# An expert with 96 slots instead of 128, in a two-layer mixer with a top-2 mixture of experts

## The chip, the cores and the metric

The kernel runs on one core of one Trainium2 chip. The metric is device microseconds of one execution; the median of three executions is given with the lowest and the highest.

## The reference

256 tokens and 256 context tokens of width 1024 go through two layers. Each layer mixes tokens (window attention beside a chunked mLSTM) and then channels: layer 0 by a dense SwiGLU of width 2816, layer 1 by a mixture of eight such SwiGLUs. All is float32. The part that the change touches is the mixture:

```python
N_EXPERTS, TOP_K, FFN_DIM = 8, 2, 2816

def swiglu(t, w1, w3, w2):
    return (jax.nn.silu(t @ w1) * (t @ w3)) @ w2

def moe_swiglu(h, w_router, b_router, w1, w3, w2):
    t = h.reshape(-1, shp[-1])                       # 256 x 1024
    logits = (t @ w_router).astype(jnp.float32) + b_router
    top_v, top_i = lax.top_k(logits, TOP_K)
    top_w = jax.nn.softmax(top_v, axis=-1)
    combine = sum over the two of one_hot(top_i) * top_w
    y = sum over e of combine[:, e] * swiglu(t, w1[e], w3[e], w2[e])
```

Each token uses two of eight experts, so 512 places fall to the eight, 64 to each on the mean.

## The kernel before

**Precision.** Every float32 operand of a large product is kept as two fp32r tiles, H (rounded) and L (the rest). `mm3` does three matmuls for one product: aH with bH, aH with bL, aL with bH. Weights come from HBM in blocks of 1 MB (`raw`), and `_split_tile` makes H on ScalarE (L123) and L on VectorE or GpSimd (L124). All matmuls go through `Timed.matmul` (L227) and `Timed.transpose` (L231), so they share those two lines; the tile names tell them apart. In these names the second operand is the stationary one: `ps_mm<-H,X` streams the weight tile H past the stationary tile X.

**The weights' order.** The program is first run once without a chip to log the order in which blocks are used; then `Weights` issues loads (L388 among others, on SyncE's queue) as buffers come free and splits blocks ahead of their use. The generators of a stage (`weave`, `take`) and an agenda (`soon(n, f)` puts f n beats later, `beat()` counts) set the order in which everything else is issued. Each engine then runs its own instructions in that order.

**The mixture.** After the router, `pos` holds for every token and expert the number of earlier tokens of that expert, and `A` whether the token uses it. `onehot` writes from them a matrix of 128 tokens x 128 slots: one where the token has that slot. An expert then works on its slots only:

- `gather(e0)` makes X for two experts at once: `rows_in` multiplies 128 tokens' rows (stationary, `tt`) with the one-hot columns of both experts (`Pt`, 2 x 128 columns streamed) for each of 8 chunks of the width, in bank `ps_t` (the first gather in several banks), and ScalarE and VectorE scale it and split it to XH and XL (L1593 to L1595). Pair 0 is gathered ahead of the experts, pairs 2, 4 and 6 inside the odd experts.
- `expert` computes the two first products with the slots as stationary columns: for six blocks of 512 columns (the last 256) of w1 and w3, 8 chunks x `mm3` into `ps_mm`. `finish` takes silu (L1618) and the product (L1619); some beats after, `later` transposes the result, `sa`, 128 columns at a time into `ps_t` (L231), and copies it to hH (ScalarE, L1633) and hL (VectorE, L1634). Then 22 chunks of w2 are multiplied with hH and hL (stationary) into two banks `ps_s`.
- the result is scaled (`ys`, L1666), split (`y`), and `combine` spreads it to the tokens with the transposed one-hot matrix `PTm` (L1562, made in `slots_t`), into the running sum `yacc` (L1679). The last expert does the same in the outer `finish`, and `result` normalizes and stores.

Work of one expert is issued under that of another: the gather of the next pair, the transposes and the scatter stand between the matmuls of w1, w3 and w2 in TensorE's queue.

**The general path.** Should an expert have more than 128 tokens, a block behind the test below runs a loop over all experts for slots 128 to 255 and normalizes again:

```python
    ncnt = nc.values_load(cnt[0:1, 0:1], min_val=0, max_val=T)
    with tc.If(ncnt > cap):
```

Of the kernel before, what the change touches and what calls it, by code (L numbers as in the profile page):

```python
# [8 lines left out]
F32 = mybir.dt.float32  # L9
# [4 lines left out]
OP = mybir.AluOpType  # L14
# [254 lines left out]

def emit(ctx, tc, I, out, order=None, log=None, dbg=None, stop=None, cap=128):  # L270
    nc = tc.nc
# [1140 lines left out]
    for tag, key in zip(("hH", "hL"), HK):  # L1412
        W.add_pool(mo, 1, lambda k, key=key: k == key, (tag, NF * 128))
    W.add_pool(mo, RAW2, late)
# [58 lines left out]
    Pt = ap_.tile([128, 1024], F32R, tag="aL0", name="Pt")  # L1473
    Pp = [Pt[:, i * 512:(i + 1) * 512].rearrange("p (b e q) -> p b e q", b=2, e=2) for i in range(2)]
    W.add_pool(ap_, 1, late, ("aL1", 2048, True))
# [68 lines left out]
    PTm = cst.tile([128, 2, T], F32R, tag="sqacc", name="PTm")  # L1544

    def onehot(dst, b, pcol, acol, shift=0):
        if shift:
            V.tensor_scalar(dst, iota, float(shift), pcol, op0=OP.add, op1=OP.is_equal)
# [7 lines left out]
    def slots_t(e0):  # L1556
        t = bank("t")
        for e in (e0, e0 + 1):
            for b in range(2):
                PE.transpose(t[:, (e - e0) * T + b * 128:(e - e0) * T + (b + 1) * 128],  # L1560
                             Pp[e0 // 2 % 2][:, b, e - e0].bitcast(F32), ident)
        soon(1, lambda: V.tensor_copy(PTm, t.rearrange("p (e t) -> p e t", e=2)))  # L1562

# [33 lines left out]
    def gather(e0):  # L1597
        XH, XL = pair_tile()
        if e0:
            for e in (e0, e0 + 1):  # L1600
                for b in range(2):
                    place(e, b)
                yield
        for j in range(8):
            p = bank("t" if e0 else ("mm", "s", "t", "mm", "s", "t", "f", "mm")[j])
            rows_in(j, p[:, :T], lambda b: Pp[e0 // 2 % 2][:, b], XH[:, j], XL[:, j], e0 == 0 and j % 2 == 1)
            yield
        for q in range(2):
            XE[e0 + q] = (XH[:, :, q], XL[:, :, q])

    def expert(xe, getw, scatter):
# [3 lines left out]
        def finish(fb, pa, pb):  # L1615
            c0, wd = EB[fb]
            sa = tmp("sa", 512)
            act(sa[:, :wd], pa[:, :wd], AF.Silu)  # L1618
            soon(1, lambda: V.tensor_tensor(sa[:, :wd], sa[:, :wd], pb[:, :wd], op=OP.mult))  # L1619

            def later():
                if not hh:
                    for nm in ("hH", "hL"):
                        t = mo.tile([128, NF * 128], F32R, tag=nm, name=nm, bufs=1)
# [6 lines left out]
                src = t[:, :wd].rearrange("p (q s) -> p q s", s=128)  # L1631
                d = hH[:, f0:f0 + wd // 128]
                act(d, src, AF.Copy)  # L1633
                soon(1, lambda: V.tensor_tensor(hL[:, f0:f0 + wd // 128], src, d.bitcast(F32), op=OP.subtract))  # L1634
            soon(NL, later)

        for fb, (c0, wd) in enumerate(EB):
            pp = []
            for nm in ("exp_w1", "exp_w3"):
                p = bank("mm")  # L1640
                pp.append(p)
# [7 lines left out]
            finish(fb, *pp)  # L1649
        y = [bank("s"), bank("s")]  # L1650
        for f in range(NF):
# [5 lines left out]
            yield  # L1657
        yt = mo.tile([128, NF * 128], F32R, tag="hH", name="y", bufs=1)
        yH, yL = yt[:, :D], yt[:, D:2 * D]

        if scatter is None:
            return y, (yH, yL)
        for half in range(2):
            r = slice(half * 512, (half + 1) * 512)
            ys = tmp("ys", 512)
            soon(Y0 + half, lambda r=r, ys=ys, p=y[half]: V.tensor_tensor(ys, p, rows["g"][:, r], op=OP.mult))  # L1666
            soon(Y0 + 1 + half, lambda r=r, ys=ys: act(yH[:, r], ys, AF.Copy))
            soon(Y0 + 2 + half, lambda r=r, ys=ys: V.tensor_tensor(yL[:, r], ys, yH[:, r].bitcast(F32), op=OP.subtract))
        scatter(yH, yL)

    def combine(PT, ccol):
        def sc(yH, yL):
            def go(b):
                for half in range(2):
                    r = slice(half * 512, (half + 1) * 512)
                    p = bank("t")
                    PE.matmul(p, PT[:, b * 128:(b + 1) * 128], yH[:, r], start=True, stop=False)
                    PE.matmul(p, PT[:, b * 128:(b + 1) * 128], yL[:, r], start=False, stop=True)
                    soon(1, lambda p=p, r=r: V.scalar_tensor_tensor(yacc[:, b, r], p, ccol(b), yacc[:, b, r],  # L1679
# [51 lines left out]
    def finish(PT, ccol, y, yy):  # L1731
        drain()
        yH, yL = yy
        hs = [slice(half * 512, (half + 1) * 512) for half in range(2)]
        ys = [tmp("ys", 512) for _ in hs]
        for q, r in enumerate(hs):
            V.tensor_tensor(ys[q], y[q], rows["g"][:, r], op=OP.mult)
            act(yH[:, r], ys[q], AF.Copy)
# [3 lines left out]
        for b, q in ((0, 0), (1, 0), (0, 1), (1, 1)):  # L1742
            p = ps[b, q] = bank("t" if q == 0 else "mm")
            tok = PT[:, b * 128:(b + 1) * 128]
            PE.matmul(p, tok, yH[:, hs[q]], start=True, stop=False)
            PE.matmul(p, tok, yL[:, hs[q]], start=False, stop=True)
# [58 lines left out]
    with tc.If(ncnt > cap):  # L1805
        ec = mo.tile([128, 1], F32, name="ec")
        V.memset(ec, -1.0)
        with tc.For_i(0, NE, 1) as ei:
            V.tensor_scalar(ec, ec, 1.0, None, op0=OP.add)
            sel = wk.tile([128, NE], F32, tag="sel", name="sel", bufs=1)  # L1810
            V.tensor_scalar(sel, iota[:, :NE], ec, None, op0=OP.is_equal)
            pc = wk.tile([128, 3, 2], F32, tag="pc", name="pc", bufs=1)
            for q, src in enumerate((pos, A, cmb)):
                for b in range(2):
                    jk = wk.tile([128, NE], F32, tag="jk", name="jk", bufs=2)
                    V.tensor_tensor(jk, src[:, b], sel, op=OP.mult)
                    V.tensor_reduce(pc[:, q, b:b + 1], jk, axis=AX.X, op=OP.add)
            P2 = Pt[:, 0:256].rearrange("p (b q) -> p b q", b=2)
            PT2 = Pt[:, 256:512]
            for b in range(2):  # L1820
                onehot(P2[:, b], b, pc[:, 0, b:b + 1], pc[:, 1, b:b + 1], cap)
            t = bank("t")
            for b in range(2):
                PE.transpose(t[:, b * 128:(b + 1) * 128], P2[:, b].bitcast(F32), ident)
            V.tensor_copy(PT2, t[:, :T])
            XH, XL = pair_tile()
            for j in range(8):
                beat()
                rows_in(j, bank("s")[:, :128], lambda b: P2[:, b], XH[:, j, 0], XL[:, j, 0])
            loaded = {}  # L1830

            def getw(key, sub):
                nm = key[0]
                if sub == 0:
                    raw = rawp.tile([128, 2048], F32, tag="raw", name="rawo", bufs=3)
                    w = I[nm][0][bass.ds(ei, 1)]
                    if nm == "exp_w2":
                        src = w[:, key[1] * 256:(key[1] + 1) * 256, :]
                        nk, wd, per = 2, 1024, 1
                    else:  # L1840
                        c0, wd = EB[key[1]]
                        nk = 4 if wd == 512 else 8
                        per = nk // 2
                        src = w[:, key[2] * 512:key[2] * 512 + nk * 128, c0:c0 + wd]
                    rv = raw.rearrange("p (k c) -> p k c", k=nk)
                    nc.sync.dma_start(rv, src.rearrange("e (k p) c -> p (e k) c", p=128))
                    loaded["v"] = (rv, per, wd)
                rv, per, wd = loaded["v"]
                return W._split_tile(None, sub3(per, wd, lambda _: rv[:, sub * per:(sub + 1) * per, :]), "o")
            drain()  # L1850
            for _ in expert((XH[:, :, 0], XL[:, :, 0]), getw, combine(PT2, lambda b: pc[:, 2, b:b + 1])):
                beat()
            drain()
        final_rows()
# [92 lines left out]
```

## Time and profile before

| | |
|---|---|
| median of 3 runs | 1686.85 us (1686.64 to 1687.09) |
| profiled execution | 1688.09 us, span 1686.3 us |
| granted TensorE clock, mean | 0.991 |
| busy: TensorE, its weight loads, VectorE, ScalarE, GpSimd | 97%, 83%, 78%, 62%, 7% of the span |
| read from HBM | 404.38 MB, of it 264 loads of 1 MB of expert weights |
| expert stage | from about 880 to 1670 us |

A row of the timeline has the start, the time to the end, the engine, the line, the operation, what it writes and reads, the stationary shape as rows*columns and the streamed shape, and a count. Matmuls are pipelined, so the time from the start of one to the start of the next (the step) is shorter than the duration; loads of stationary columns ("PEld", LDWEIGHTS) run beside the stream of the matmul before. A row with a count covers several instructions from the first start to the last end. Waits and idle times name the instruction that ended them.

### The profile page before, as it was taken

The numbers are of one execution on the slowest core, as the hardware profiler recorded it, in microseconds if no ns is written. First come the engines' busy times: TensorE is split into PE (matmuls) and PEld (weight loads), VectorE is DVE, ScalarE is ACT, GpSimd is POOL, SyncE is SP. The second block draws the span as 40 slices with busy tenths as digits, with TensorE's granted clock in tenths as the row PEclk, the third lists the DMA queues.
The fourth block names the chain that finished last, engine by engine and source line by source line (L and its number), as shares of the span: only waits on it lengthen the run. The fifth ranks groups of instructions, "written<-read, shape, count | busy, mean of one in ns | idle before, by whom it ended". The sixth has DMA issues, their size and how long they took to land.

```text
span 1686.3 us, 24379 instructions
## 1 busy us (share of the span) xinstructions
PE 1641.4 (97%) x9202; PEld 1391.6 (83%) x9202; DVE 1315.7 (78%) x1994; ACT 1040.7 (62%) x1546; POOL 122.1 (7%) x171
## 2 busy tenths in 40 slices
PE   8989999999999999999999999999999999999996
PEld 6779789998888889898988888888888888888885
DVE  3585568887666736785668999999999899898987
ACT  5544676632223224647647777877787777877775
POOL 2330111100000000303110000000000000000001
PEclk8999999999999999999999999999999999999998
DMA  9322544575557823441187999999999999999990
GB/s 307 110 75 76 176 150 151 160 239 176 174 184 265 281 75 121 157 126 50 60 293 266 356 354 351 342 349 357 364 351 320 359 369 353 346 333 358 357 337 27
DMA packets 222637, 407.08 MB, mean 241 GB/s; under 512 B 9776, under 2 KB 106288, under 8 KB 222512
## 3 DMA queue, kind: packets, MB, share of 16 engines
q1 hardware_dynamic: 220464, 404.38, 69.1%
q8 instruction: 74, 1.21, 0.3%
q10 hardware_dynamic: 2048, 1.07, 0.2%
q14 instruction: 51, 0.42, 0.1%
HBM read 404.38 MB, written 1.05 MB: 240 GB/s over the span
## 4 chain that ended last, share of the span: by engine, by line
PE 85%; DVE 8%; ACT 3%; issue 1%; POOL 1%; DMA 1%; POOLq 0%; ACTq 0%; DVEq 0%
PE ps_mm L227 55%; PE ps_s L227 16%; PE ps_t L227 4%; PE ps_f L227 3%; PE ps_t L231 3%; DVE L L124 2%; PE ps_o L227 2%; PE ps_sb L227 1%; DVE ca L783 1%; ACT H L123 1%; POOL t L892 1%; DMA tok<-in_x 0%; DVE xn L539 0%; DMA raw<-in_w_in 0%; PE ps_mm L1470 0%
## 5 line engine op out<-in xcount | busy, mean ns | idle before, releaser
L123 ACT ACTIVATE H<-raw 128x1024 fp32r<-128x1024 f32 (+1 forms) x676 | 702.3, 1050 | 385.8 <-PE ps_mm L227 295.3
L124 DVE TENSOR_TENSOR L<-raw,H 128x1024 fp32r<-128x1024 f32 (+1 forms) x671 | 801.5, 1219 | 135.8 <-ACT H L123 130.9
L227 PE MATMUL ps_mm<-H,X 128*128 128x512 f32 (+1 forms) x1536 | 461.0, 379 | 0.0
L227 PEld LDWEIGHTS ps_mm<-H,X 128*128 128x128 f32 x1536 | 280.6, 188 | 56.2
L227 PE MATMUL ps_mm<-L,X 128*128 128x512 f32 (+1 forms) x768 | 288.4, 376 | 0.0
L227 PE MATMUL ps_mm<-aH,H 128*128 128x512 f32 (+1 forms) x752 | 259.2, 347 | 2.3 <-ACT aH L542 2.3
L227 PE MATMUL ps_mm<-aL,H 128*128 128x512 f32 (+1 forms) x752 | 257.3, 343 | 3.3 <-DVE aL L545 1.4
L227 PE MATMUL ps_mm<-aH,L 128*128 128x512 f32 (+1 forms) x752 | 257.0, 342 | 0.0
L227 PEld LDWEIGHTS ps_mm<-L,X 128*128 128x128 f32 x768 | 144.7, 188 | 27.6
L227 PEld LDWEIGHTS ps_mm<-aH,H 128*128 128x128 f32 x752 | 142.6, 190 | 21.4 <-ACT aH L542 2.5
L227 PEld LDWEIGHTS ps_mm<-aL,H 128*128 128x128 f32 x752 | 143.1, 190 | 20.5 <-DVE aL L545 2.3
L227 PEld LDWEIGHTS ps_mm<-aH,L 128*128 128x128 f32 x752 | 142.8, 190 | 16.5 <-issue 0.4
L227 PE MATMUL ps_s<-H,hH 128*128 128x512 f32 x352 | 140.4, 399 | 0.0
L227 PE MATMUL ps_s<-L,hH 128*128 128x512 f32 x352 | 139.0, 395 | 0.0
L227 PE MATMUL ps_s<-H,hL 128*128 128x512 f32 x352 | 138.7, 394 | 0.0
L611 DVE SCALAR_TENSOR_TENSOR macc<-raw,csil,macc 128x1024 f32<-128x1024 f32 x70 | 87.6, 1280 | 4.4 <-DMA raw<-in_w_mod 3.9
L227 PEld LDWEIGHTS ps_s<-H,hL 128*128 128x128 f32 x352 | 66.0, 188 | 15.9
L227 PEld LDWEIGHTS ps_s<-H,hH 128*128 128x128 f32 x352 | 66.1, 188 | 14.2
L227 PEld LDWEIGHTS ps_s<-L,hH 128*128 128x128 f32 x352 | 66.1, 188 | 13.9
L227 PE MATMUL ps_mm<-fH,H 128*128 128x512 f32 (+1 forms) x224 | 77.2, 345 | 0.0
L227 PE MATMUL ps_mm<-fL,H 128*128 128x512 f32 (+1 forms) x224 | 77.1, 344 | 0.0
L227 PE MATMUL ps_mm<-fH,L 128*128 128x512 f32 (+1 forms) x224 | 77.0, 344 | 0.0
(356 smaller groups left out, 2128.0 us busy)
## 6 DMA issues: line engine op xcount, KB each, us to landing
raw<-in_exp_w SPq DMA_DIRECT2D x264, 1024.0 KB, 5.9
raw<-in_w_mod SPq DMA_DIRECT2D x48, 1024.0 KB, 5.7
raw<-in_ffn_w SPq DMA_DIRECT2D x34, 1024.0 KB, 5.4
raw<-in_w_in SPq DMA_DIRECT2D x18, 1024.0 KB, 5.6
raw<-in_w_out SPq DMA_DIRECT2D x12, 1024.0 KB, 5.2
raw<-in_ffn_w SPq DMA_DIRECT2D x8, 768.0 KB, 4.4
tok<-in_ctx SPq DMA_DIRECT2D x2, 512.0 KB, 4.8
tok<-in_x SPq DMA_DIRECT2D x2, 512.0 KB, 7.2
```

Of the source, the lines that this page charges most:

```text
L123: nc.scalar.activation(h, src, AF.Copy)
L124: eng.tensor_tensor(l, src, h.bitcast(F32), op=OP.subtract)
L227: return self.eng.matmul(o, a, b, **kw)
L231: return self.eng.transpose(o, a, i)
L611: V.scalar_tensor_tensor(a, raw[:, q], c, a, op0=OP.mult, op1=OP.add)
L783: V.scalar_tensor_tensor(a, u[:, j:j + T], vc[:, w + 4 * j + chunk:w + 4 * j + chunk + 1], a, op0=OP.mult, op1=OP.add)
L892: G.tensor_tensor(t1, t1, t2, op=OP.add)
```

## The change

`cap`, the number of slots of an expert, goes from 128 to 96 in everything that has slots: the one-hot matrices, the gathered X, the partitions of `sa`, `y` and the accumulating banks, the transposed hH and hL and the space of their tiles (22 x 96 elements instead of 22 x 128), the transposed one-hot matrix. The general path runs for a count above 96, and there in two rounds, slots 96 to 191 and 192 to 287. The core of the diff:

```diff
-def emit(ctx, tc, I, out, order=None, log=None, dbg=None, stop=None, cap=128):
+def emit(ctx, tc, I, out, order=None, log=None, dbg=None, stop=None, cap=96):
...
-        W.add_pool(mo, 1, lambda k, key=key: k == key, (tag, NF * 128))
+        W.add_pool(mo, 1, lambda k, key=key: k == key, (tag, NF * cap))
...
+    slot = iota[:, :cap]
     def onehot(dst, b, pcol, acol, shift=0):
...
-            V.tensor_scalar(dst, iota, pcol, acol, op0=OP.is_equal, op1=OP.mult)
+            V.tensor_scalar(dst, slot, pcol, acol, op0=OP.is_equal, op1=OP.mult)
...
-        X = cst.tile([128, 2, 8, 2, 128], F32R, tag="xT", name="X")
+        X = cst.tile([128, 2, 8, 2, cap], F32R, tag="xT", name="X")
...
-            rows_in(j, p[:, :T], lambda b: Pp[e0 // 2 % 2][:, b], XH[:, j], XL[:, j], e0 == 0 and j % 2 == 1)
+            rows_in(j, p[:, :2 * cap], lambda b: Pp[e0 // 2 % 2][:, b], XH[:, j], XL[:, j], e0 == 0 and j % 2 == 1)
...
-            sa = tmp("sa", 512)
+            sa = tmp("sa", 512)[:cap]
...
-                    PE.transpose(t[:, q * 128:(q + 1) * 128], sa[:, q * 128:(q + 1) * 128], ident)
+                    PE.transpose(t[:, q * cap:(q + 1) * cap], sa[:, q * 128:(q + 1) * 128], ident[:cap, :cap])
...
-                p = bank("mm")
+                p = bank("mm")[:cap]
...
-        y = [bank("s"), bank("s")]
+        y = [bank("s")[:cap], bank("s")[:cap]]
...
-                    PE.matmul(p, PT[:, b * 128:(b + 1) * 128], yH[:, r], start=True, stop=False)
+                    PE.matmul(p, PT[:cap, b * 128:(b + 1) * 128], yH[:, r], start=True, stop=False)
...
     with tc.If(ncnt > cap):
-        V.memset(ec, -1.0)
-        with tc.For_i(0, NE, 1) as ei:
+        for shift in range(cap, T, cap):
+            V.memset(ec, -1.0)
+            with tc.For_i(0, NE, 1) as ei:
```

Up to the test of the general path each engine has the same instructions in the same order; shapes alone differ. (Lines from `slot` on stand two further down, those in the general path three.) On TensorE, around the first block's transposes, H and L being the split weights and X the stationary slots; before:

```order
L227 MATMUL ps_mm<-L_9054,X 128x512
L227 MATMUL ps_mm<-H_9053,X 128x512
L231 MATMUL ps_t<-kc,sa 128x128 x4
L227 MATMUL ps_mm<-H_9064,X 128x512
L227 MATMUL ps_mm<-L_9065,X 128x512
```

and now:

```order
L227 MATMUL ps_mm<-L_9054,X 96x512
L227 MATMUL ps_mm<-H_9053,X 96x512
L231 MATMUL ps_t<-kc,sa 128x96 x4
L227 MATMUL ps_mm<-H_9064,X 96x512
L227 MATMUL ps_mm<-L_9065,X 96x512
```

The shape is that of the output: the products lose partitions and keep their 512 streamed columns, the transposes lose streamed columns. On ScalarE at the same place, where `sa` is the silu and hH the copy of the transposed block; before:

```order
L1618 ACTIVATE sa<-ps_mm 128x512
L123 ACTIVATE H_9053<-raw_8424 128x1024
L123 ACTIVATE H_9064<-raw_8426 128x1024
L123 ACTIVATE H_9079<-raw_8426 128x1024
L123 ACTIVATE H_9090<-raw_8434 128x1024
L1633 ACTIVATE hH<-ps_t 128x512
```

and now:

```order
L1620 ACTIVATE sa<-ps_mm 96x512
L123 ACTIVATE H_9053<-raw_8424 128x1024
L123 ACTIVATE H_9064<-raw_8426 128x1024
L123 ACTIVATE H_9079<-raw_8426 128x1024
L123 ACTIVATE H_9090<-raw_8434 128x1024
L1635 ACTIVATE hH<-ps_t 128x384
```

The silu loses partitions, the copy loses a quarter of its elements, the splits between them stay.

More of the change, by code (lines that the diff above doesn't have):

```diff
@@ L1473, in emit @@
     Pt = ap_.tile([128, 1024], F32R, tag="aL0", name="Pt")
-    Pp = [Pt[:, i * 512:(i + 1) * 512].rearrange("p (b e q) -> p b e q", b=2, e=2) for i in range(2)]
+    Pp = [Pt[:, i * 512:i * 512 + 4 * cap].rearrange("p (b e q) -> p b e q", b=2, e=2) for i in range(2)]
     W.add_pool(ap_, 1, late, ("aL1", 2048, True))
@@ L1623, in later @@
                     for nm in ("hH", "hL"):
-                        t = mo.tile([128, NF * 128], F32R, tag=nm, name=nm, bufs=1)
+                        t = mo.tile([128, NF * cap], F32R, tag=nm, name=nm, bufs=1)
                         hh.append(t.rearrange("p (f s) -> p f s", f=NF))
@@ L1657, in expert @@
             yield
-        yt = mo.tile([128, NF * 128], F32R, tag="hH", name="y", bufs=1)
-        yH, yL = yt[:, :D], yt[:, D:2 * D]
+        yt = mo.tile([128, NF * cap], F32R, tag="hH", name="y", bufs=1)
+        yH, yL = yt[:cap, :D], yt[:cap, D:2 * D]
         if scatter is None:
@@ L1664, in expert @@
             r = slice(half * 512, (half + 1) * 512)
-            ys = tmp("ys", 512)
-            soon(Y0 + half, lambda r=r, ys=ys, p=y[half]: V.tensor_tensor(ys, p, rows["g"][:, r], op=OP.mult))
+            ys = tmp("ys", 512)[:cap]
+            soon(Y0 + half, lambda r=r, ys=ys, p=y[half]: V.tensor_tensor(ys, p, rows["g"][:cap, r], op=OP.mult))
             soon(Y0 + 1 + half, lambda r=r, ys=ys: act(yH[:, r], ys, AF.Copy))
@@ L1676, in go @@
                     p = bank("t")
-                    PE.matmul(p, PT[:, b * 128:(b + 1) * 128], yH[:, r], start=True, stop=False)
-                    PE.matmul(p, PT[:, b * 128:(b + 1) * 128], yL[:, r], start=False, stop=True)
+                    PE.matmul(p, PT[:cap, b * 128:(b + 1) * 128], yH[:, r], start=True, stop=False)
+                    PE.matmul(p, PT[:cap, b * 128:(b + 1) * 128], yL[:, r], start=False, stop=True)
                     soon(1, lambda p=p, r=r: V.scalar_tensor_tensor(yacc[:, b, r], p, ccol(b), yacc[:, b, r],
@@ L1734, in finish @@
         hs = [slice(half * 512, (half + 1) * 512) for half in range(2)]
-        ys = [tmp("ys", 512) for _ in hs]
+        ys = [tmp("ys", 512)[:cap] for _ in hs]
         for q, r in enumerate(hs):
-            V.tensor_tensor(ys[q], y[q], rows["g"][:, r], op=OP.mult)
+            V.tensor_tensor(ys[q], y[q], rows["g"][:cap, r], op=OP.mult)
             act(yH[:, r], ys[q], AF.Copy)
@@ L1743, in finish @@
             p = ps[b, q] = bank("t" if q == 0 else "mm")
-            tok = PT[:, b * 128:(b + 1) * 128]
+            tok = PT[:cap, b * 128:(b + 1) * 128]
             PE.matmul(p, tok, yH[:, hs[q]], start=True, stop=False)
@@ L1806, in emit @@
         ec = mo.tile([128, 1], F32, name="ec")
-        V.memset(ec, -1.0)
-        with tc.For_i(0, NE, 1) as ei:
[L1809 to L1813, printed above, removed]
-                for b in range(2):
[L1815 to L1853, printed above, removed]
@@ new lines, in emit, with getw @@
+        for shift in range(cap, T, cap):
+            V.memset(ec, -1.0)
+            with tc.For_i(0, NE, 1) as ei:
+                V.tensor_scalar(ec, ec, 1.0, None, op0=OP.add)
+                sel = wk.tile([128, NE], F32, tag="sel", name="sel", bufs=1)
+                V.tensor_scalar(sel, iota[:, :NE], ec, None, op0=OP.is_equal)
+                pc = wk.tile([128, 3, 2], F32, tag="pc", name="pc", bufs=1)
+                for q, src in enumerate((pos, A, cmb)):
+                    for b in range(2):
+                        jk = wk.tile([128, NE], F32, tag="jk", name="jk", bufs=2)
+                        V.tensor_tensor(jk, src[:, b], sel, op=OP.mult)
+                        V.tensor_reduce(pc[:, q, b:b + 1], jk, axis=AX.X, op=OP.add)
+                P2 = Pt[:, 0:2 * cap].rearrange("p (b q) -> p b q", b=2)
+                PT2 = Pt[:, 256:512]
+                for b in range(2):
+                    onehot(P2[:, b], b, pc[:, 0, b:b + 1], pc[:, 1, b:b + 1], shift)
+                t = bank("t")
+                for b in range(2):
+                    PE.transpose(t[:cap, b * 128:(b + 1) * 128], P2[:, b].bitcast(F32), ident)
+                V.tensor_copy(PT2[:cap], t[:cap, :T])
+                XH, XL = pair_tile()
+                for j in range(8):
+                    beat()
+                    rows_in(j, bank("s")[:, :cap], lambda b: P2[:, b], XH[:, j, 0], XL[:, j, 0])
+                loaded = {}
+                def getw(key, sub):
+                    nm = key[0]
+                    if sub == 0:
+                        raw = rawp.tile([128, 2048], F32, tag="raw", name="rawo", bufs=3)
+                        w = I[nm][0][bass.ds(ei, 1)]
+                        if nm == "exp_w2":
+                            src = w[:, key[1] * 256:(key[1] + 1) * 256, :]
+                            nk, wd, per = 2, 1024, 1
+                        else:
+                            c0, wd = EB[key[1]]
+                            nk = 4 if wd == 512 else 8
+                            per = nk // 2
+                            src = w[:, key[2] * 512:key[2] * 512 + nk * 128, c0:c0 + wd]
+                        rv = raw.rearrange("p (k c) -> p k c", k=nk)
+                        nc.sync.dma_start(rv, src.rearrange("e (k p) c -> p (e k) c", p=128))
+                        loaded["v"] = (rv, per, wd)
+                    rv, per, wd = loaded["v"]
+                    return W._split_tile(None, sub3(per, wd, lambda _: rv[:, sub * per:(sub + 1) * per, :]), "o")
+                drain()
+                for _ in expert((XH[:, :, 0], XL[:, :, 0]), getw, combine(PT2, lambda b: pc[:, 2, b:b + 1])):
+                    beat()
+                drain()
```

8 lines of the change are left out of this document (4 added, 4 removed).

## The prediction

> **What bounds the kernel now.** I read the page's busy shares and slices first, then the stages around the experts, then the waits inside them, then the timeline of TensorE row by row.
>
> ```profile
> PE 1641.4 (97%) x9202; PEld 1391.6 (83%) x9202; DVE 1315.7 (78%) x1994; ACT 1040.7 (62%) x1546; POOL 122.1 (7%) x171
> PE   8989999999999999999999999999999999999996
> DMA  9322544575557823441187999999999999999990
> ```
>
> From slice 21 of 40 on (about 880 us) TensorE and the DMA engines both read 9. That is the expert stage, nearly half of the span. Two full rows don't say which of the two sets the pace; the next table does (columns: stretch, length, busy time of each engine with its instructions, granted TensorE clock, DMA share, GB/s).
>
> ```profile
> 840.00:860.00 20.00, 20.00 (x179) 20.00 (x178) 11.99 (x21) 9.39 (x14) 0.00 (x0) 1.00 1.04 387
> 1100.00:1200.00 100.00, 100.00 (x466) 81.91 (x465) 92.24 (x90) 78.30 (x84) 0.00 (x0) 1.00 1.00 354
> 1645.00:1665.00 20.00, 20.00 (x87) 16.12 (x86) 18.13 (x17) 15.54 (x15) 0.00 (x0) 1.00 0.00 1
> ```
>
> Among the experts the DMA moves 354 GB/s; before them, with many loads queued, 387. It could go 9% faster. From 1645 us on it has nothing left to move, and TensorE is as full as before, at 20 us over 87, 230 ns an instruction: the step that its streams also have beside full transfers (below). So TensorE sets the pace, at full granted clock. VectorE is at 92% and would be next. The waits from 980 to 1670 us agree (who waited, for whom: us in total, times, longest); the last row is the DMA queue's own, to 1640:
>
> ```profile
> ACT H L123 <- PE ps_mm L227: 67.1, 169, 1.6
> ACT hH L1633 <- PE ps_t L231: 31.0, 42, 0.8
> ACT H L123 <- DMA raw<-in_exp_w: 7.2, 13, 1.3
> SPq L388 <- DVE L L124: 481.5, 189, 3.7
> ```
>
> ScalarE waits for TensorE to give buffers back, hardly ever for a transfer, and the transfers wait for buffers. Any nanosecond taken off a TensorE instruction there comes off the end, until VectorE's 8% are used up.
>
> **The 512-column matmuls.** An expert's slots are the stationary columns of mm3; the expert's weights stream past them, 512 columns at a time, 256 in the last block. Six blocks of w1 and w3 over 8 chunks and 22 chunks of w2 make 2976 streams of 512 and 384 of 256. The change takes a quarter of the stationary columns and none of the streamed ones. First and last of ten streams in a row, the same with 256 columns, the same two in the dense layer, and one pair in plain f32 (start us, us to the end):
>
> ```profile
> 959.18 0.39 PE L227 MATMUL ps_s<-H,hL 128*128 128x512 f32 x1
> ...
> 961.27 0.40 PE L227 MATMUL ps_s<-H,hL 128*128 128x512 f32 x1
> 942.04 0.28 PE L227 MATMUL ps_mm<-L,X 128*128 128x256 f32 x1
> ...
> 943.10 0.28 PE L227 MATMUL ps_mm<-L,X 128*128 128x256 f32 x1
> 419.79 0.39 PE L227 MATMUL ps_mm<-aH,H 128*128 128x512 f32 x1
> ...
> 420.92 0.39 PE L227 MATMUL ps_mm<-aH,L 128*128 128x512 f32 x1
> 250.72 0.28 PE L227 MATMUL ps_f<-aL,H 128*128 128x256 f32 x1
> ...
> 251.43 0.28 PE L227 MATMUL ps_f<-aL,H 128*128 128x256 f32 x1
> 177.93 0.60 PE L227 MATMUL ps_sb<-QM_c,KM_c 128*128 128x256 f32 x2
> ```
>
> Start to start: 2.09 us over 9 steps is 232 ns in the experts; 1.06 over 9 is 118 with 256 columns; 1.13 over 5 is 226 in the dense layer, and 0.71 over 6 is 118 there. Twice the columns cost about twice the time, so the streamed columns pay nearly all of it. The dense pair gives (226-118)/256 = 0.42 ns a column; 512 of them are 216, which leaves 16 ns of 232 that the columns don't explain. (The plain f32 pair, 0.60 less one matmul's 0.38, steps at 217 with a full stationary load beside it.) The load itself is beside the stream:
>
> ```profile
> L227 PEld LDWEIGHTS ps_s<-H,hH 128*128 128x128 f32 x352 | 66.1, 188 | 14.2
> L227 PEld LDWEIGHTS ps_f<-raw,csil 128*32 128x32 f32 x320 | 8.9, 110 | 8.8 <-issue 3.8 <-PE ps_t L227 0.3
> ```
>
> 128 stationary columns take 188 ns, 32 take 110: 0.81 a column, so 96 take about 162. Both end before the stream beside them does. I therefore cost the 2976 streams at nothing. The ends are -4 ns each (a quarter of the 16, if those belong to the load) and, above, the rivals. The load's 26 ns are hidden by the stream; were it uncovered, it would be a gain too.
>
> **Transposes of sa.** Each expert turns its 22 chunks in `later` (176 in all). The slots are the streamed side there, 128 before and 96 now; the loaded side keeps 128 columns.
>
> ```profile
> 935.88 0.60 PE L231 MATMUL ps_t<-kc,sa 128*128 128x128 f32 x4
> 98.19 0.23 PE L231 MATMUL ps_f<-kc,Fc 36*128 36x36 f32 x1
> 98.25 0.23 PE L231 MATMUL ps_f<-kc,g 36*128 36x36 f32 x1
> 98.31 0.23 PE L231 MATMUL ps_f<-kc,Fc 36*128 36x36 f32 x1
> L231 PE MATMUL ps_t<-kc,sa 128*128 128x128 f32 x176 | 27.0, 272 | 0.0
> ```
>
> Four take 0.60 and one 0.272, so they step at 109 ns. With 36 streamed columns (and a load of 128) the step is 60. Plain f32 at 256 columns steps at 217 and at 128 at 109, in proportion; 96 would step at 82, above the 60 that 36 columns still cost. 176 x 27 = -4.7 us. A straight line from 109 to 60 would give 92 and -3.0; a load that sets the 109 would give 0.
>
> **Gathers.** The three later gathers stream 256 columns of Pp, now 192, past 128 columns of token rows: 3 pairs x 8 chunks x 4 = 96.
>
> ```profile
> 1056.61 0.63 PE L227 MATMUL ps_t<-Pt,tt 128*128 128x256 f32 x4
> 98.47 0.19 PEld L227 LDWEIGHTS ps_mm<-aH,H 128*128 128x128 f32 x1
> 98.58 0.19 PEld L227 LDWEIGHTS ps_mm<-aL,H 128*128 128x128 f32 x1
> 879.40 1.05 PE L227 MATMUL ps_t<-Pt,tt 128*128 128x256 f32 x4
> 880.25 0.94 PE L227 MATMUL ps_f<-Pt,tt 128*128 128x256 f32 x4
> 877.70:880.80 3.10, 3.10 (x16) 3.10 (x16) 2.67 (x7) 2.75 (x7) 0.00 (x0) 0.50 0.72 273
> ```
>
> They step at (0.63-0.28)/3 = 117. Where nothing streams, two loads of 128 columns start 110 apart, so the load holds the step near 110: 96 x 7 = -0.7 us (ends 0 and, in proportion to columns, -2.8). The first gather runs 16 of its 32 at half the granted clock (0.50 in the last row), four from 879.40 to 880.25, 213 each; again the load may hold them: -0.4 us (ends 0 and 16 x 53 = -0.85).
>
> **The rest.** The 384 streams of 256: 0, since the dense layer's 118 is no shorter; if the load's 110 is what holds 118, it falls to at best 0.42 x 256 = 108, -10 each, -3.8. Copies of the transposed block shrink from 512 to 384 elements:
>
> ```profile
> L1633 ACT ACTIVATE hH<-ps_t 128x512 fp32r<-128x512 f32 x35 | 21.0, 599 | 27.1 <-PE ps_t L231 27.1
> L1633 ACT ACTIVATE hH<-ps_t 128x256 fp32r<-128x256 f32 x7 | 2.7, 385 | 3.9 <-PE ps_t L231 3.9
> L1634 DVE TENSOR_TENSOR hL<-ps_t,hH 128x512 fp32r<-128x512 f32 x35 | 23.9, 684 | 0.0
> ```
>
> At (599-385)/256 = 0.84 ns an element ScalarE saves 0.11 us on each of 40, 4 us in all, and VectorE about as much; neither is on the path, so nothing, but VectorE's spare share grows, which covers TensorE's gain. sa, ys, y and the scatter lose partitions, not elements, and cost the same; so the tail after the last matmul stays. No transfer and no instruction before the final test is added or moved. The second round's code lies behind a branch that isn't taken: the reference's own inputs send 66, 60, 83, 65, 51, 56, 67 and 64 tokens to the eight experts, and 83 fits 96.
>
> Sum: 0 - 4.7 - 0.7 - 0.4 = -5.8 us. The profiled execution took 1688.09 us (span 1686.3), 1.24 above the median of 1686.85; 1682.3 on its scale is 1681.0 on the median's. Ends of this case: 0 and -4.7-2.8-0.85-3.8 = -12.2, so 1675 to 1687.
>
> **Rivals.**
> - The 16 ns belong to the stationary load and shrink with its columns. For it: plain f32, whose columns stream more slowly, shows no such rest, and the dense layer holds 226 where the experts hold 232 without a cause that I can name. -4 x 2976 = -12 us, at 226 -18, on top of -5.8: 1663 to 1669.
> - The load, not the stream, sets the 109 of the transposes, and 232 stays: about -1 us, 1686, no change.
> - Slower: TensorE stops whenever the number of stationary columns it uses changes. The 32-column row above idles 3.8 us ("issue") over 20 groups of 16, 0.19 us per group, on coming from 128 columns. Some 100 groups of transposes, gathers and scatters use 128 columns amid 96: 100 x 0.19 = +19 us, 1700 after the gains. It decides from 31 stops on. Against it: the 32-column matmuls there write four separate column groups, 96 columns start at column 0 like 128. The Trainium skill's page "TensorEngine Tiling (Array Packing)" says in "Key Properties" that changing the tiling mode drains TensorE, and lists under "Available Configurations" 128, 64 and 32 columns, not 96; the row agrees for 32, no run here shows 96.
> - The load gets longer below 128 columns. If the 110 ns step were a shortened one, four times as fast as the plain, 96 columns would hold a stream for 4 x 0.75 x 110 = 330 ns: 98 x 2976 + 212 x 384 = +373 us, 2054. The two load rows speak against it: 32 columns at 110 and 128 at 188 leave no room for that. (The Trainium skill's page "TensorE: Matmul & The Clock Gate", section "Weight-path perf modes", has such a fast load for exactly 128 weights of a type other than FP32; by it the loss would hang on how fp32r counts, and the trace doesn't show a fast load.)
> - The change doesn't do what it says: a count above 96 would run 16 more expert passes of (1670-880)/8 = 99 us, +1580.
>
> **How the numbers follow.** First case 0.51, of which 0.43 is a gain above 3.4 us; shrinking rest 0.25; nothing shrinks 0.11; stops at changes of width, or a step that settles higher than 232, 0.11; longer load 0.01; general path 0.01. 0.2% is 3.4 us, about what the runs can tell from no change. Faster 0.43 + 0.25 = 0.68, slower 0.13, same 0.19. The range takes in the first three, 1661 to 1689, and leaves out the slow ones.
>
> **What the profile after would show.** Right: the same 2976 streams at 232 ns, transposes of sa at 82, gathers near 110, loads of 96 columns near 162, VectorE's share about as before, no idle time of TensorE among the experts. Streams at 226 to 229 would show the first rival; idle "issue" time next to transposes and gathers, or longer steps there, the slower one; loads over 188 the one after. I am wrong if the step of the 512-column streams moves by over 2 ns either way, since 2976 of them outweigh everything else.

## The result, and the profile after

The changed kernel takes 1675.69 us in the median of three runs (1675.45 to 1678.47), against 1686.85 before: a ratio of 0.994, 95% interval 0.9927 to 0.9954. It is faster by 11.2 us where 5.8 were forecast. Its profiled execution is the one of 1675.69 us. The page:

```profile
span 1673.9 us, 24379 instructions
PE 1627.2 (97%) x9202; PEld 1304.6 (78%) x9202; DVE 1309.5 (78%) x1994; ACT 1035.3 (62%) x1546; POOL 122.3 (7%) x171
PE   8989999999999999999999999999999999999996
DMA  9322544565558824431086999999999999999990
```

The number of instructions is the same on every engine, and only the weight loads' share falls by much, from 83% to 78%. Two stretches, one among the experts and one in which there is nothing left to move (columns as in the prediction):

```profile
1100.00:1200.00 100.00, 100.00 (x471) 72.03 (x470) 92.88 (x91) 78.46 (x84) 0.00 (x0) 1.00 1.00 363
1635.00:1655.00 20.00, 20.00 (x88) 14.00 (x87) 16.31 (x14) 13.12 (x13) 0.00 (x0) 1.00 0.00 1
```

TensorE is full as before and goes through 471 instructions where it went through 466; the DMA follows, 363 GB/s for 354; VectorE goes from 92% to 93%. The waits from 980 to 1660 us say the same as before: ScalarE waits for TensorE to give buffers back, hardly ever for a transfer.

```profile
ACT H L123 <- PE ps_mm L227: 61.4, 160, 1.5
ACT hH L1635 <- PE ps_t L231: 26.8, 42, 0.7
ACT H L123 <- DMA raw<-in_exp_w: 9.0, 19, 1.3
```

The difference of the two spans, 12.4 us, falls apart at two rows: the first stream of the first expert and the last of the last. Of before:

```profile
881.51 0.39 PE L227 MATMUL ps_mm<-H,X 128*128 128x512 f32 x1
...
1669.02 0.39 PE L227 MATMUL ps_s<-H,hL 128*128 128x512 f32 x1
```

Of after:

```profile
878.73 0.40 PE L227 MATMUL ps_mm<-H,X 128*96 128x512 f32 x1
...
1656.02 0.40 PE L227 MATMUL ps_s<-H,hL 128*96 128x512 f32 x1
```

The expert stage took 787.5 us and now takes 777.3: 10.2 less. The rest is 2.8 us ahead of it and +0.6 behind it. The next table adds up the steps (start of a matmul to start of the next) of all matmuls of the stage, by what they are. It is worked out from the starts in the two traces.

```
steps in the expert stage                  before              after             after - before
plain 512-column streams, 2796             651.82 (233.1 ns)   647.48 (231.6)    -4.34 us
256-column streams, 376                     44.27 (117.7)       44.33 (117.9)    +0.06
transposes of sa, within a group, 128       13.91 (108.7)       10.64 (83.1)     -3.27
the last of each group, 48                   1.35 (28.2)         1.32 (27.5)     -0.03
the stream right after each group, 48       15.22 (317.0)       13.84 (288.4)    -1.38
later gathers, 96                           11.54 (120.2)       10.20 (106.2)    -1.34
scatter of y, 56                            13.98 (249.6)       14.12 (252.1)    +0.14
all others                                  35.41               35.36            -0.05
sum                                        787.50              777.29           -10.21
```

How a group of transposes takes part in two of these lines is seen in the timeline of after:

```profile
932.18 0.40 PE L227 MATMUL ps_mm<-H,X 128*96 128x512 f32 x1
932.42 0.49 PE L231 MATMUL ps_t<-kc,sa 96*128 96x96 f32 x4
932.70 0.45 PE L227 MATMUL ps_mm<-H,X 128*96 128x512 f32 x1
932.98 0.40 PE L227 MATMUL ps_mm<-L,X 128*96 128x512 f32 x1
```

and of before, where the group itself starts at 935.88 (row in the prediction):

```profile
936.24 0.48 PE L227 MATMUL ps_mm<-H,X 128*128 128x512 f32 x1
936.55 0.40 PE L227 MATMUL ps_mm<-L,X 128*128 128x512 f32 x1
```

Four transposes hold the next stream off for 0.36 us before and 0.28 after, and the second stream behind them starts 0.31 us after the first before, 0.28 after. The groups of instructions that belong to it, in after:

```profile
L227 PEld LDWEIGHTS ps_s<-H,hH 128*96 128x96 f32 x352 | 56.8, 161 | 21.7
L231 PE MATMUL ps_t<-kc,sa 96*128 96x96 f32 x176 | 22.4, 245 | 0.0
L1635 ACT ACTIVATE hH<-ps_t 128x384 fp32r<-128x384 f32 x40 | 19.7, 493 | 26.1 <-PE ps_t L231 26.1
L1636 DVE TENSOR_TENSOR hL<-ps_t,hH 128x384 fp32r<-128x384 f32 x40 | 22.0, 550 | 0.0
```

The loads take 161 ns, the transposes 245 where they took 272, the copies 0.11 and 0.13 us less each.

### The profile page after: what moved, and what is told of

Its sections match the earlier page's. It is cut to its first block, busy times and chain, and to the rows that moved or that the text cites. A ratio compares the mean times of both kernels' runs of the same rounds, so it can differ in the third digit from the quotient of the medians.

```text
span 1673.9 us, 24379 instructions
## 1 busy us (share of the span) xinstructions
PE 1627.2 (97%) x9202; PEld 1304.6 (78%) x9202; DVE 1309.5 (78%) x1994; ACT 1035.3 (62%) x1546; POOL 122.3 (7%) x171
## 4 chain that ended last, share of the span: by engine, by line
PE 87%; DVE 7%; ACT 3%; POOL 1%; issue 1%; DMA 1%; POOLq 0%; ACTq 0%; DVEq 0%
PE ps_mm L227 57%; PE ps_s L227 17%; PE ps_t L227 4%; PE ps_f L227 3%; PE ps_t L231 3%; PE ps_o L227 2%; DVE L L124 2%; PE ps_sb L227 1%; DVE ca L783 1%; ACT H L123 1%; POOL t L892 1%; DMA tok<-in_x 0%; DVE xn L539 0%; DMA raw<-in_w_in 0%; DMA vc<-in_cols 0%
## 5 line engine op out<-in xcount | busy, mean ns | idle before, releaser
L227 PE MATMUL ps_mm<-H,X 128*96 128x512 f32 (+1 forms) x1536 | 457.6, 376 | 0.0
L227 PEld LDWEIGHTS ps_mm<-H,X 128*96 128x96 f32 x1536 | 242.6, 161 | 87.1
L227 PE MATMUL ps_mm<-L,X 128*96 128x512 f32 (+1 forms) x768 | 287.9, 375 | 0.0
L227 PEld LDWEIGHTS ps_mm<-L,X 128*96 128x96 f32 x768 | 124.0, 161 | 43.3 <-DVE L L124 0.2
L227 PE MATMUL ps_s<-H,hH 128*96 128x512 f32 x352 | 139.5, 396 | 0.0
L227 PE MATMUL ps_s<-H,hL 128*96 128x512 f32 x352 | 138.6, 394 | 0.0
L227 PE MATMUL ps_s<-L,hH 128*96 128x512 f32 x352 | 138.3, 393 | 0.0
L227 PEld LDWEIGHTS ps_s<-H,hL 128*96 128x96 f32 x352 | 56.8, 161 | 24.8
L227 PEld LDWEIGHTS ps_s<-L,hH 128*96 128x96 f32 x352 | 56.8, 161 | 22.0
L227 PEld LDWEIGHTS ps_s<-H,hH 128*96 128x96 f32 x352 | 56.8, 161 | 21.7
```

The source lines that it names most:

```text
L227: return self.eng.matmul(o, a, b, **kw)
```

## The experiments

Two questions were open: why 2796 streams got 1.5 ns shorter each, though they stream the same columns, and what the 2.8 us ahead of the stage and the 0.6 behind it are. The theory for the first: the width of a stream's own stationary operand counts (as a load, or as columns in use). Its rivals: the tiles of the change lie at other addresses, or the step goes by filled groups of 32 columns.

### Both kernels again

No edit: the changed kernel five times beside the one before, and the one before once more for its trace.

> The changed kernel once more, in five rounds. In the two traces the stretch from the first expert matmul to the last shrank by 10.2 us (787.5 to 777.3), but 2.65 us of the 12.4 between the two spans lie ahead of the first gather, where both programs are the same. Theory A: those 2.65 us are chance, half-clock windows of TensorE in the first 30 us that fall differently from run to run; then a repeated comparison gives 9 to 10.5 us less than before on the median. Theory B: the start belongs to the change (a program of another length); then again 11 to 12.5 us less, and the first gather again near 870.7 us and not 873.3.

> The kernel before, profiled once more. Theory A (chance at the start): the first gather falls anywhere from 870 to 874 us, and the expert stage has 787.5 us again, with the 512-column streams stepping at 233.1 ns on the mean to within 0.2. Theory B: first gather at 873.3 again. If the expert stage itself differs by more than 1 us from 787.5, the step is not a property of the program, and the whole account of the streams is open.

Measured: 1678.09 us after (1676.48 to 1680.19), 1686.85 before (11 runs, 1685.47 to 1688.11); ratio 0.995, interval 0.9936 to 0.9963. The second trace of before has 1684.49 us. The gain is 8.8 us here and was 11.2 before, and the intervals overlap; 8.8 lies just under the 9 to 10.5 of theory A and well under theory B. The stage is the same to 0.1 us in both traces of each kernel: 787.50 and 787.50 before, 777.29 and 777.20 after. What differs is the start, where the programs are alike. The first 40 us of before and of its repetition, then of after and of its repetition (columns as above; the last three are granted clock, DMA share and GB/s):

```profile
0.00:40.00 40.00, 33.55 (x221) 26.72 (x222) 15.29 (x38) 19.38 (x43) 9.40 (x10) 0.87 0.97 305
```

```profile
0.00:40.00 40.00, 33.48 (x244) 26.26 (x244) 16.71 (x41) 21.40 (x47) 10.55 (x12) 0.96 1.02 319
```

```profile
0.00:40.00 40.00, 32.35 (x240) 25.05 (x244) 17.05 (x41) 21.31 (x47) 10.22 (x12) 0.96 1.02 319
```

```profile
0.00:40.00 40.00, 33.92 (x223) 26.96 (x224) 15.82 (x40) 19.90 (x44) 9.40 (x10) 0.87 0.99 308
```

Each kernel has one trace with a mean clock of 0.87 and 221 to 223 matmuls there, and one with 0.96 and 240 to 244. The first gather starts at 873.3 and 875.3 us in those of 0.87, at 869.7 and 870.7 in those of 0.96. The stage begins at 881.5 and 877.9 us in the two traces of before, and at 878.7 and 881.3 in those of after. So a start moves by 2.5 to 3.6 us between two runs of one kernel, and the 2.8 us ahead of the stage in the first pair of traces are within that. What the change gives is the stage's -10.2, and the end's +0.6.

### The tiles at their old places

96 slots, with every tile that has slots as long as at 128:

```diff
-        W.add_pool(mo, 1, lambda k, key=key: k == key, (tag, NF * cap))
+        W.add_pool(mo, 1, lambda k, key=key: k == key, (tag, NF * 128))
...
-        X = cst.tile([128, 2, 8, 2, cap], F32R, tag="xT", name="X")
-        return X[:, 0], X[:, 1]
+        X = cst.tile([128, 2, 8, 2, 128], F32R, tag="xT", name="X")
+        return X[:, 0, :, :, :cap], X[:, 1, :, :, :cap]
...
-                        t = mo.tile([128, NF * cap], F32R, tag=nm, name=nm, bufs=1)
+                        t = mo.tile([128, NF * 128], F32R, tag=nm, name=nm, bufs=1)
```

> 96 slots, but every tile of slots keeps the size and the stride that it had with 128 (X, hH, hL, y, the one-hot matrices), so that every operand begins where it began before. Theory 1 (the narrower load shortens the step): streams of 512 columns at 231.6 ns as in the changed kernel, expert stage 777 us. Theory 2 (the operands' places set the step): streams at 233.1 again, expert stage 777.3 + 4.4 = 782 us, with only the transposes' 3.3 and the gathers' 1.3 us left of the gain.

Measured: 1678.11 us (1676.15 to 1679.43), ratio 0.9953, interval 0.9938 to 0.9968. The stage, first and last stream:

```profile
878.44 0.39 PE L227 MATMUL ps_mm<-H,X 128*96 128x512 f32 x1
...
1656.50 0.40 PE L227 MATMUL ps_s<-H,hL 128*96 128x512 f32 x1
```

It is 778.1 us, 0.8 more than after and 9.4 less than before. The plain streams step at 231.9 ns. So putting the tiles back moves the step by 0.3 ns, and the other 1.2 of the 1.5 stay: the places are not what took these.

### Only the second product narrow

Gathers, X, w1 and w3 use 128 slots again; `sa`, the transposes, w2 and the scatter stay at 96.

```diff
-            rows_in(j, p[:, :2 * cap], lambda b: Pp[e0 // 2 % 2][:, b], XH[:, j], XL[:, j], e0 == 0 and j % 2 == 1)
+            rows_in(j, p[:, :T], lambda b: Pp[e0 // 2 % 2][:, b], XH[:, j], XL[:, j], e0 == 0 and j % 2 == 1)
...
-                p = bank("mm")[:cap]
+                p = bank("mm")[:xH.shape[2]]
...
-            act(sa[:, :wd], pa[:, :wd], AF.Silu)
-            soon(1, lambda: V.tensor_tensor(sa[:, :wd], sa[:, :wd], pb[:, :wd], op=OP.mult))
+            act(sa[:, :wd], pa[:cap, :wd], AF.Silu)
+            soon(1, lambda: V.tensor_tensor(sa[:, :wd], sa[:, :wd], pb[:cap, :wd], op=OP.mult))
```

> The gathers and the products with w1 and w3 have 128 stationary slots again, all after them (transposes, w2, scatter) 96. Theory 1 (the load's own width): the 1920 streams of w1 and w3 step at 233 to 233.5 ns as before, the 1056 of w2 at 231.4; expert stage 777.3 + 3.9 + 1.3 (gathers) = 782.5 us. Theory 3 (the step is a matter of how the streams fall in with each other, whatever the width): both kinds near one value, anything from 227 to 234, and the expert stage off 782.5 by over 1.5 us.

Measured: 1681.48 us (1679.85 to 1683.41), ratio 0.9967, interval 0.9956 to 0.9979. First and last stream:

```profile
881.64 0.39 PE L227 MATMUL ps_mm<-H,X 128*128 128x512 f32 x1
...
1663.72 0.40 PE L227 MATMUL ps_s<-H,hL 128*96 128x512 f32 x1
```

The stage is 782.1 us. The plain streams of 512 columns step at 233.5 ns in w1 and w3 (before 233.3, after 231.7) and at 231.2 in w2 (232.8 and 231.3). So the streams with 128 stationary columns went back and those with 96 stayed, in one program: the step goes with the stream's own stationary width. The trace shows one thing more. The stream after a group of transposes steps at 316 ns where it has 128 stationary columns (32 of them) and at 288 where it has 96 (16), though the transposes are the same, with 96 streamed columns at 82.9 ns. That -1.38 us of the table belongs to the stream's load and not to the transposes: a load that is 27 ns shorter (188 to 161), and uncovered there. The kernels of the next section agree: with 120, 112 and 84 stationary columns the same step is 308, 301 and 278 ns and the load 181, 174 and 152, so that from 128 to 84 the step stays 126 to 129 ns longer than the load.

### Other widths

The number of slots alone, once each, but with the space of hH, hL and y kept large enough for their other users: 112, 120 and 94.

```diff
-def emit(ctx, tc, I, out, order=None, log=None, dbg=None, stop=None, cap=96):
+def emit(ctx, tc, I, out, order=None, log=None, dbg=None, stop=None, cap=112):
...
-                        t = mo.tile([128, NF * cap], F32R, tag=nm, name=nm, bufs=1)
+                        t = mo.tile([128, max(NF * cap, 2048)], F32R, tag=nm, name=nm, bufs=1)[:, :NF * cap]
```

> 112 slots in all of the routing, otherwise the changed kernel. Theory 1 (the narrower load shortens the step, by its columns): streams of 512 columns at 232.4 ns, halfway from 233.1 to 231.6; transposes of sa at 96 ns (in proportion to the streamed columns: 0.86 ns each, 109 at 128, 83 at 96); expert stage 782.4 us, halfway from 787.5 to 777.3. Theory 3 (a width has its own step, not in order): the streams outside 231.6 to 233.1, the stage off by over 1.5 us.

> 120 slots, otherwise the changed kernel. Until now: streams of w1 and w3 at 233.3 ns with 128 stationary columns, 231.6 with 112, 231.7 with 96, 230.5 with 84. If the step falls evenly with the columns (0.06 ns each from 128 to 84), 232.8 here. If it goes by whole groups of 32 columns that are filled (4 at 128, 3 at 112 and 96, 2 at 84), 231.6 here. Transposes of sa at 103 ns either way.

> 94 slots, two fewer than the changed kernel; the tiles of hH, hL and y are 2068 elements. If the step falls evenly, the streams of w1 and w3 take 231.1 to 231.6 ns, as with 96; if it goes by filled groups of 32 columns, 230.5 as with 84, and the expert stage loses 3 us or more against 777.3 (streams 2976 x 1.0, transposes 0.2).

And 84, the same edit, timed in five rounds:

> 84 slots (the largest count of these inputs is 83), the tiles of hH, hL and y kept at 2048 elements because y needs them. Theory 1: streams at 231.1 ns (12 columns less at 0.047 ns each), -1.7 us; transposes at 72 ns, -1.4 us; gathers held by the load of 128 columns, -0.3 at most; expert stage 774 us. The general path has three rounds of code instead of two: if the code behind the branch costs 0.6 us a round at the end (17.25 us from the last expert matmul to the end with one round, 17.85 with two), 18.4 us there. In all 2.5 to 3 us faster than the changed kernel, about 10 to 11 us faster than before. Theory 3: streams anywhere from 227 to 235, so -10 to +10 us.

Measured, with the other kernels of 96 and 128 columns (worked out from the starts in the traces; the last column counts the streams, in stretches of eleven and more without another instruction between, by the mean step of their stretch; streams at half the granted clock and those right behind a group of transposes are left out of the last column, and the former out of the mean step too):

```
columns            time us   stage us  plain 512-column step   transposes   under 231 / 231-232 / 232-233 / 233 and more
128 (before)       1686.85   787.50    233.1 ns                108.7 ns        0 /   44 / 1357 / 1519
120                1682.87   782.50    231.9                   103.1         230 /  955 / 1663 /   72
112                1676.92   779.12    231.2                    96.5         993 / 1705 /   79 /  143
96 (after)         1675.69   777.29    231.6                    83.1         458 / 1170 / 1101 /  191
96, old places     1678.11   778.06    231.9                    82.9
94                 1678.10   778.58    231.6                    81.4
84                 1671.92   773.24    230.5                    73.1        2153 /  657 /   83 /    0
```

The transposes go by columns, 0.81 ns for each. The step of the streams falls too, 2.6 ns over the 44 columns from 128 to 84, but not evenly: 112 columns step shorter than 96, and at 112 the expectation (232.4 ns, stage 782.4 us) was missed by 1.2 ns and 3.3 us. Of the two rules that the next expectations set against each other, neither holds for both widths. With 120 columns w1 and w3 step at 232.0 ns, nearer to the 231.6 of three filled groups of 32 than to the 232.8 of an even fall. With 94 they step at 231.7, near the even fall and 1.2 ns above the 230.5 of two filled groups.

A width isn't all that counts. The streams of w1 and w3 differ between the even and the odd experts of one program, though they have the same shapes:

```
slots            128     120     112      96      94      84
even experts   233.4   231.7   231.8   231.6   231.2   229.7 ns
odd experts    233.2   232.3   231.2   231.9   232.3   231.1
```

Even and odd experts have different halves of X, and the gathers of the next pair stand among the odd ones; which of these counts was not separated. Since each width also moves the tiles, the table can't say how much of the unevenness belongs to the width. The mean also hides unlike stretches, which the timeline of after shows in one expert's w2, with the same shapes; first and last of 15 streams, then of 21:

```profile
946.38 0.39 PE L227 MATMUL ps_s<-H,hH 128*96 128x512 f32 x1
...
949.65 0.39 PE L227 MATMUL ps_s<-H,hL 128*96 128x512 f32 x1
...
955.63 0.39 PE L227 MATMUL ps_s<-H,hH 128*96 128x512 f32 x1
...
960.20 0.40 PE L227 MATMUL ps_s<-H,hL 128*96 128x512 f32 x1
```

3.27 us over 14 steps is 234 ns, 4.57 over 20 is 229. On the whole, fewer stationary columns make the short stretches more. What sets a stretch's step isn't settled by these runs: the places of the tiles moved it by 0.3 ns, the widths by up to 2.6, and the dense layer steps at 227 with 128 columns in every kernel.

84 slots are the best of these kernels: 1671.92 us (1670.99 to 1672.47) against 1685.64 of before in nine runs beside it, ratio 0.9915, interval 0.9902 to 0.9929. That is 13.7 us faster, where 10 to 11 were expected. First and last stream, and the stretch ahead of and around the first:

```profile
879.55 0.63 PE L227 MATMUL ps_mm<-H,X 128*84 128x512 f32 x1
...
1652.79 0.40 PE L227 MATMUL ps_s<-H,hL 128*84 128x512 f32 x1
```

```profile
874.80:881.60 6.80, 6.80 (x29) 6.04 (x29) 4.19 (x12) 4.16 (x12) 0.00 (x0) 0.50 0.33 125
```

The stage begins here at half the granted clock, its first streams at 427 ns, which costs it 1.0 us. The traces of 94 and 64 slots have the same, 1.2 and 1.3 us, and the others don't; without it 94 slots have 777.4 us, as after.

It beats both kernels, and hangs on the largest count of these inputs, 83; one token more on that expert is covered, and with two the general path would run.

### 64 slots, for the stops

The prediction's slower rival says that TensorE stops where the number of stationary columns in use changes. The kernel with 64 slots has groups that change the columns alone (gathers, 128 amid 64) and groups that change the rows (transposes and scatters, 64 rows amid 128). How the program sets the array for them stands in the expectation; no view of the profile shows it.

```diff
-def emit(ctx, tc, I, out, order=None, log=None, dbg=None, stop=None, cap=96):
+def emit(ctx, tc, I, out, order=None, log=None, dbg=None, stop=None, cap=64):
...
-    with tc.If(ncnt > cap):
+    with tc.If(ncnt > T - 1):
```

> 64 slots; tokens beyond the 64th of an expert are left out, and the test of the general path is set so that it never runs. 64 stationary columns and 64 rows are no longer given the whole array: the program sets 128x64 and 64x128 for them, between matmuls on 128x128. If TensorE stops at each change of that setting, as it did ahead of the 32-column matmuls (0.19 us a group), the 100 groups of transposes, gathers and scatters cost about 19 us: expert stage 771 + 19 = 790 us, with idle time of TensorE next to them. If it doesn't, theory 1 gives streams at 230.1 ns, transposes at 55 to 63, expert stage 771 us.

Measured, one run: 1684.57 us, the stage 784.6. The timeline at the first group of transposes, as shown of after above:

```profile
934.96 0.40 PE L227 MATMUL ps_mm<-H,X 128*64 128x512 f32 x1
935.28 0.46 PE L231 MATMUL ps_t<-kc,sa 64*128 64x64 f32 x4
935.67 0.44 PE L227 MATMUL ps_mm<-H,X 128*64 128x512 f32 x1
935.95 0.39 PE L227 MATMUL ps_mm<-L,X 128*64 128x512 f32 x1
```

The step into the group is 0.32 us instead of 0.24, and the four transposes hold the next stream off for 0.39 instead of 0.28, though they stream fewer columns. A scatter, and a gather with the streams beside it:

```profile
986.26 0.40 PE L227 MATMUL ps_mm<-H,X 128*64 128x512 f32 x1
986.59 1.19 PE L227 MATMUL ps_t<-y,PTm 64*128 64x512 f32 x4
```

```profile
1052.59 0.39 PE L227 MATMUL ps_s<-H,hL 128*64 128x512 f32 x1
1052.82 0.56 PE L227 MATMUL ps_t<-Pt,tt 128*128 128x128 f32 x4
1053.21 0.40 PE L227 MATMUL ps_s<-H,hH 128*64 128x512 f32 x1
```

The step into the scatter is 0.33 us, the one into the gather 0.23, as between streams. The waits of the weight loads from 880 to 1660 us, and the loads of the streams, the transposes and the gathers:

```profile
PEld ps_mm L227 <- issue: 6.3, 20, 0.4
PEld ps_t L227 <- issue: 5.8, 14, 0.4
PEld ps_t L231 <- issue: 4.5, 13, 0.4
```

```profile
L227 PEld LDWEIGHTS ps_s<-H,hH 128*64 128x64 f32 x352 | 47.4, 135 | 30.9
L231 PEld LDWEIGHTS ps_t<-kc,sa 64*128 64x128 f32 x176 | 14.4, 137 | 18.1 <-DVE L L124 10.2 <-issue 4.5 <-PE ps_s L227 3.4
L227 PEld LDWEIGHTS ps_t<-Pt,tt 128*128 128x128 f32 x104 | 15.9, 195 | 3.4
```

The stops are real at 64 slots, but not at every change of the columns, as the rival has it. They stand at the groups whose rows change. On the mean the step into a group of transposes is 305 ns (214 in after), the first one inside it 112 where the later ones have 62, and the last 152 (28); the loads ahead of the 48 groups stand idle for 18.1 us. The 14 scatters have a step of 325 ns into them (232 in after). The 24 gathers, which go from 64 stationary columns to 128 and back, have 232 ns into them and 234 behind, and no idle time that the view names. So going from 64 stationary columns to 128 and back, with 128 rows in both, doesn't stop TensorE. By these steps a stop costs about 0.26 us in each of 62 groups, 16 us in all. The stage shows less against the 771 us that were expected without stops, 13.6 us, since the plain streams step at 229.3 ns instead of 230.1; 1.3 of the 13.6 are the half clock at its start. Within a group the transposes step at 62 ns, as expected (55 to 63).

The three rows of the waits are absent at 96, where the weight loads wait for "issue" nowhere in that window. The Trainium skill's page "TensorEngine Tiling (Array Packing)", section "Key Properties", says that a change of the tiling mode drains TensorE; the groups with 64 rows agree, the gathers amid 64 columns show no drain, and the rows of after show none at 96.

### One round in the general path

The code of the second round is left out of the block that doesn't run.

```diff
-        for shift in range(cap, T, cap):
+        for shift in range(cap, cap + 1, cap):
```

> The changed kernel with one round of the general path instead of two (slots 96 to 191 only; none of it runs here). If the second round's code behind the branch makes the end longer, 17.25 us from the last expert matmul to the end as before, 0.6 less than the changed kernel; if the end is longer for another reason (96 rows in the last scatter), 17.85 again. Expert stage 777.3 us in either case.

Measured, one run: 1675.22 us, span 1673.4; the stage 777.18. The last row of the chain of waits in before, in after and in this kernel:

```profile
1679.69 0.72 ACT z L1712
```

```profile
1666.69 0.72 ACT z L1714
```

```profile
1666.77 0.72 ACT z L1714
```

From the last stream (1669.02, 1656.02, 1656.11) to the end of that row it is 11.39, 11.39 and 11.38 us, the same. From there to the end of the span it is 5.90, 6.51 and 5.95. So the 0.6 us lie behind the last arithmetic, and come and go with the second round's code, which is skipped. At 84 slots, with three rounds, the last stream starts 17.89 us ahead of the end, with two 17.90 (before 17.30): a third round adds nothing. Why the second does stays open.

## Why the prediction was right, and where not

The time, 1675.69, lies within the range, and the mechanism was that of the first case (the transposes and gathers gave 6.0 us where 5.8 were forecast) and a part of its first rival (the streams gave 4.3). Without the luck of the start the change is worth -10.2 + 0.6 = -9.6 us, where -5.8 stood; the two measured gains of medians, 11.2 and 8.8, have it between them.

- **The bound.** Right: TensorE is full, its steps are what moved the stage, VectorE and the DMA followed.
- **The streams of 512 at nothing.** This is the term that was mis-sized: -4.34 us, 1.55 ns for each of 2796, where 0 was taken and -4 ns each was the end. The working asked only whether the load ends before the stream does, and it does (161 and 188 ns of 232). The step goes with the stationary width all the same, as the run with only the second product narrow shows; by what means stays open. The first rival, that a quarter of the rest of 16 ns goes, was right in its sign and 2.6 times too large. The mean step moved by less than 2 ns, the prediction's own bound for being wrong.
- **Transposes of sa.** The size was right, -4.7, the working half: 128 of the 176 step within a group, at 83 ns (82 forecast), for -3.27. The last of each group was hidden before and is now; the missing -1.38 is the load of the stream behind it, which the prediction had covered everywhere and which is uncovered there. That the two together come to the forecast size is luck.
- **Later gathers.** -1.34 for -0.7. Of the four steps of a group, three went from 122 to 113 ns and stay at 112 with 84 slots and with 64 (168 and 128 streamed columns): there the load holds the step near 110, as the prediction had it, and that is -0.64 us. The first step wasn't held. It fell from 116 to 87, and goes on to 78 and 58 with 84 and 64 slots, by the streamed columns; that is the other -0.70 us.
- **First gather.** 0 for -0.4. Three groups of four at half the granted clock in after:

```profile
875.69 1.05 PE L227 MATMUL ps_s<-Pt,tt 128*128 128x192 f32 x4
876.54 1.05 PE L227 MATMUL ps_t<-Pt,tt 128*128 128x192 f32 x4
877.39 1.05 PE L227 MATMUL ps_f<-Pt,tt 128*128 128x192 f32 x4
```

 They stand 0.85 us apart, as with 256 columns before, 213 ns each, and the step is 213 at half clock with 168 and 128 streamed columns too. So the streamed columns don't set it; the load of 128 columns, the same in all of them, fits, as the prediction had it for the lower end. At full clock the steps fell from about 119 to 111, and from the first gather to the first stream it is 8.20 us before and 8.07 after.
- **Streams of 256 and copies at nothing.** Right: 117.7 and 117.9 ns; the copies got shorter, and TensorE's loads waited for none of them.
- **The tail.** 0 was forecast and 0.6 us came, from code that doesn't run.
- **The rivals.** Stops: not at 96. At 64 slots they come with a change of rows, and not with one from 64 to 128 columns alone. The 3.8 us of the 32-column row are 12 idle times of 0.32 us, not 20 of 0.19. These matmuls have 128 rows like their neighbours, and in before the step into them is 0.31 us behind the plain f32 matmuls (0.22 between those), so there the columns do stop TensorE. What decides it stays open. Longer load: refuted, 188, 161 and 135 ns at 128, 96 and 64 columns. General path: not run, the stage ends at 1656. "The load sets the transposes": refuted by 83 ns, and by 73 at 84 columns.

## What to carry to other kernels

Cost a step by what follows it as well: a short instruction between long ones may hide its own last part and uncover the next one's load. A term of thousands of equal instructions is not nothing because each is covered; put the smallest difference that the rows can't exclude on it and multiply. Before counting a gain of a few microseconds, compare the stages in which the two programs differ, each from its own first instruction, since here the start alone moved by 2.5 to 3.6 us from run to run.

## What was not expected of the hardware

- The step of a stream of 512 columns goes with the width of its stationary operand, 233.1 ns at 128 columns and 230.5 at 84, though a load of 188 ns lies beside the stream; and it changes from stretch to stretch, 229 and 234 ns with the same shapes. The mechanism is open.
- With 64 slots TensorE stopped at groups with 64 stationary rows amid 128, 0.26 us a group, and not at gathers with 128 stationary columns amid 64 (a step of 232 ns into them, 234 behind).
- TensorE's granted clock in the first 40 us was 0.87 or 0.96 in the traces of the same program, and the expert stage began 3.6 us later (before) and 2.5 us later (after) in the trace with 0.87.
- Code behind a branch that isn't taken can cost time: 0.6 us at the end of the program for a second round, and none for a third.
